# A streaming encoder step on one core: the state recurrence moved ahead of the output tables, and regrouped

## The chip, the cores and the metric

The kernel runs on one core of a Trainium2 chip. The metric is the device time of one execution in microseconds; 879.08 us is the median of three runs of the kernel before (878.42 to 879.44). One more execution was taken by the hardware profiler, and every row below comes from that one.

## What is computed

One layer of a hybrid encoder, for 512 frames of a new stream (the prompt) and 16 frames of each of 8 running streams (the samples), 640 tokens in all. All is float32; a matrix product is made of three products of split halves (high x high, high x low, low x high).

```python
h = rmsnorm(x) @ w_in                      # 1024 x 8192: q, k, v, ga, u, gs, and two gate logits xa, xs
o = softmax(q1 k1) v - lam * softmax(q2 k2) v     # 8 heads, chunk-causal; samples also see 256 cached frames
o = rmsnorm(o) * silu(ga);  ya = o @ w_attn_proj            # "ap"
s_t = a * s_{t-1} + B u_t                  # 64 groups, 64 complex states each
y = gelu(Re(C s) + D u)
y = y * sigmoid(y @ w_glu + b)             # "gl"
ys = (y * silu(gs)) @ w_ssm_proj           # "sp"
x + (sigmoid(xa) * ya + sigmoid(xs) * ys) @ w_out           # "o0", "o1"
```

The recurrence runs by chunks of 8 frames. With a8 the eighth power of a, the state after chunk c is R[c] = R[c] + a8 * R[c-1]: 64 chunks for the prompt, in columns 25 to 88 of R (column 24 is the start), and two chunks for each sample in columns 0 to 15.

## The kernel before, in words

Weights come from DRAM in 512 KB tiles, ScalarE writes their high half (`whi`) and VectorE the rest (`wlo`), and PE multiplies. `gemm_a` makes outputs of 128 tokens by 512 columns, `gemm_b` of 128 columns by 320 tokens. The constant `ORDER` lists the products. Between their matmuls the small steps of attention and of the state space are put in, each a Python generator that yields where it waits. `Weave` is the planner: it keeps an estimated clock for each engine, asks after each group of matmuls whether a generator is due (`poll`), and `DELAY` adds a time to single steps by name. PE's order is the order of the program, planned in this way; the other engines' queues, SP's with all DMAs among them, are ordered by the framework. Engines run their own queues in order.

The state space has these steps:

- `evac_u` splits the product u (`ue`) and stores it to DRAM. `ssm_setup` computes the powers of a in tables `P1`, `P2`, the scaled B in `bbs`, and `a8`.
- `ssm_f` makes 16 tables `F` (three 512-element instructions each, on VectorE or GpSimd, whichever `lighter` finds less loaded). `ssm_in` transposes them on PE, splits them (`Wh`, `Wl`), multiplies with u and stores the chunk inputs (`so`) to `s_d`.
- `ssm_tap` makes 16 tables `E` (three 576-element instructions each, with a helper tile `Et`) and stores them to `e_d`; after each four, 16 matmuls of `E` with `bbs`, 32 columns of the array each, give the taps, which VectorE completes with D and a DMA stores to `tap_d`.
- `states` loads `s_d` into `R` and runs the recurrence; `m` are its helper tiles. `R` goes to `r_d`.
- In the output stage `out_load` brings, for each of 16 groups, `Ef`, `T` (taps), `u` and `H` (states) back; `out_split` splits them into `TO` and `Hs`; `out_mm` runs 24 matmuls (`ps_s<-TO,...`) into `yo`; after two groups `out_gelu` transposes `yo` and applies GELU to `yf`. `y_prep` splits `yf` into `yh`, `yl`, the operand of "gl".

`director` opens and closes the buffers and so sets the stages. Before, `ssm_tap` starts right after `ssm_setup`, beside `ssm_f`; `states` starts when `ssm_in` and `ssm_tap` are done, in the first half of the attention heads. When the heads' inputs and the states are done, the sample phase starts: `sample_k` and `sample_v` load cached keys (`skt`) and values (`svt`) of 512 KB each, `sample_scores` makes scores and softmax (`sw`), `sample_pv` the products with values, whose result `ob` goes to DRAM and comes back as `osm`; `samples_end` norms `osm`, transposes it on PE, multiplies it with its gates (`gaT`) and splits it into the operand of "ap" (`ogh`, `ogl`). The output stage runs beside "ap", and "gl" needs all of its result.

```python
            yield after("ssm_in", 2)                       # director: what follows the input stage
            pclose("wp", "ssm1", "fbuf")
            ...
            if hf == 0:
                yield both(after("tap"), after("att0", ST_AT))
                pclose("tape", "tapp")
                t3 = popen("t3")
                W.add(states(t3))
                yield after("att0", 4)
        yield both(both(after("q0", 5), after("q1", 5)), after("states"))
```

Of the kernel before, what the change touches and what calls it, by code (L numbers as in the profile page):

```python
# [255 lines left out]
def trunk(nc, tc, a):  # L256
# [73 lines left out]
    e_d = dram.tile([128, 64, 144], F32, name="e_d")  # L330
    tap_d = dram.tile([16, 32, 960], F32, name="tap_d")
# [431 lines left out]
    def ssm_tap(tpe):  # L763
        dT = tpe.tile([128, 4, 4], F32, name="dT")
        SP.dma_start(dT, a["dT"])
        dm = tpe.tile([128, 16], F32, name="dm")
# [3 lines left out]
        PL.memset(bbs[:, 64], 0.0)  # L770
# [6 lines left out]
        for q in range(4):  # L777
# [16 lines left out]
            for i in range(4):  # L794
                for g in range(4):
# [267 lines left out]

    def states(t3):
        def cstep(E, dst, src, n):
            sh = [128, 2, 32, n]
            m1, m2 = (t3.tile(sh, F32, name="m12", tag=f"m{n}", bufs=2) for _ in range(2))
            E.tensor_tensor(m1, a8[:, 0, :, :, None].to_broadcast(sh), R[:, :, :, src:src + n], op=OP.mult)
            E.tensor_tensor(m2, a8[:, 1, :, :, None].to_broadcast(sh), R[:, ::-1, :, src:src + n], op=OP.mult)
            E.tensor_tensor(m1, m1, m2, op=OP.add)  # L1070
            E.tensor_tensor(R[:, :, :, dst:dst + n], R[:, :, :, dst:dst + n], m1, op=OP.add)
# [3 lines left out]
        h0 = t3.tile([128, 2, 32, 8], F32, name="h0")  # L1075
        SP.dma_start(h0, a["h0"])
        W.hold()
        yield
        AC.activation(R[:, :, :, 16:24], h0, AF.Copy)
        for d in (8, 0):  # L1080
            for i in range(0, 8, 2):
                cstep(PL, d + i, d + 8 + i, 2)
            yield CHAIN
        PL.tensor_copy(h0, R[:, :, :, 0:8])
        SP.dma_start(a["ss"], h0)
# [317 lines left out]
    def director():  # L1403
# [9 lines left out]
        tpe = popen("tape")  # L1413
# [3 lines left out]
        W.add(ssm_tap(tpe))  # L1417
# [7 lines left out]
        pclose("wp", "ssm1", "fbuf")  # L1425
# [64 lines left out]
    for n, opn, cols in ORDER:  # L1490
# [17 lines left out]
        mark(n)  # L1508
        if n == X_LAST:
# [163 lines left out]
```

## Time and profile before

| what | value |
|---|---|
| median of three runs | 879.08 us |
| the profiled execution, its own time | 887.47 us |
| its span, first to last instruction | 885.7 us |
| mean granted TensorE clock | 0.987 |
| busy: PE, VectorE, ScalarE, GpSimd | 847.1, 558.9, 373.0, 253.0 us |
| DMA | 167.42 MB, mean 189 GB/s |

PE is busy when a matmul is in flight. The stages follow each other in time: v and u to about 105 us, the state-space input with the keys' products to about 237, the first four heads with the recurrence to about 370, the other heads to 523, the samples from 496 to 607, the output stage from 621 to 714, and after that the last four large products alone. The granted clock is a share of the full rate: 1.00 is 2.4 GHz.

### The profile page before, as it was taken

To read this page: it belongs to the slowest core of one execution; us is meant where nothing else is said; L and a number is where in the kernel's file an instruction comes from. 1 tells how busy PE (TensorE), PEld (TensorE's weight loads), DVE (VectorE), ACT (ScalarE), POOL (GpSimd) and SP (SyncE) were. 2 spreads that over 40 slices of the span, in tenths; PEclk is the share of its full clock that TensorE was granted. 3 is DMA by queue.
4 is the path that set the end of the run, shared out by engine and by line. 5 is a ranking of instruction groups with operands and counts; after the bars stand their busy time and mean duration, and the time that the engine had idled before them with its cause. 6 is when DMAs were issued, how large, how long until landed. Compare 5 with 4: busy or idle time off the path is not lost.

```text
span 885.7 us, 15567 instructions
## 1 busy us (share of the span) xinstructions
PE 847.1 (96%) x5692; PEld 776.9 (88%) x5692; DVE 558.9 (63%) x1267; ACT 373.0 (42%) x784; POOL 253.0 (29%) x426
## 2 busy tenths in 40 slices
PE   8999899889899989989999999999999999999998
PEld 6898889789789888767899887789999999999886
DVE  6688449886857788575667764224577755555321
ACT  6432227444236455233555544433565643422110
POOL 3734435323022996879810120000000000000000
PEclk8999899999899999999999999999999999999999
DMA  7365747564818531352585499958989763355231
GB/s 301 97 196 165 224 149 231 163 222 161 263 53 276 161 114 52 102 164 65 170 312 182 155 294 370 353 183 245 290 261 299 226 237 117 105 150 181 95 120 60
DMA packets 96445, 167.42 MB, mean 189 GB/s; under 512 B 16752, under 2 KB 54256, under 8 KB 96112
## 3 DMA queue, kind: packets, MB, share of 16 engines
q1 hardware_dynamic: 96368, 166.42, 59.1%
q8 instruction: 45, 0.74, 0.3%
q14 instruction: 32, 0.26, 0.1%
HBM read 118.45 MB, written 43.75 MB: 183 GB/s over the span
## 4 chain that ended last, share of the span: by engine, by line
PE 62%; POOL 12%; DMA 10%; DVE 10%; issue 3%; ACT 2%; SPq 1%; POOLq 0%; DVEq 0%; ACTq 0%
PE ps_mm L243 50%; POOL m L243 6%; PE ps_s L243 6%; DMA wraw<-in_wb_dram 4%; PE ps_pv L243 3%; PE ps_tp L243 3%; POOL R L243 3%; DVE wlo L243 2%; POOL rs L243 1%; ACT whi L243 1%; DMA svt<-in_cv_dram 1%; DMA H<-r_d 1%; DMA Ef<-e_d 1%; DMA u_d<-ue 1%; DVE kTl L243 1%
## 5 line engine op out<-in xcount | busy, mean ns | idle before, releaser
L243 PE MATMUL ps_mm<-xh,whi 128*128 128x320 f32 x640 | 205.5, 321 | 5.5 <-DVE ue L243 5.5
L243 PE MATMUL ps_mm<-xh,wlo 128*128 128x320 f32 x640 | 199.4, 312 | 0.0
L243 PE MATMUL ps_mm<-xl,whi 128*128 128x320 f32 x640 | 199.3, 311 | 0.0
L243 DVE TENSOR_TENSOR wlo<-wraw,whi 128x1024 fp32r<-128x1024 f32 x96 | 119.8, 1249 | 77.7 <-ACT whi L243 77.1
L243 ACT ACTIVATE whi<-wraw 128x1024 fp32r<-128x1024 f32 x96 | 101.6, 1059 | 109.7 <-PE ps_mm L243 79.6
L243 PEld LDWEIGHTS ps_mm<-xh,whi 128*128 128x128 f32 x640 | 121.9, 190 | 10.8 <-DVE ue L243 6.0
L243 PEld LDWEIGHTS ps_mm<-xl,whi 128*128 128x128 f32 x640 | 121.9, 190 | 0.8
L243 PEld LDWEIGHTS ps_mm<-xh,wlo 128*128 128x128 f32 x640 | 121.6, 190 | 0.0
L243 PE MATMUL ps_mm<-whi,xh 128*128 128x512 f32 x240 | 99.0, 412 | 0.9 <-ACT xh L243 0.9
L243 PE MATMUL ps_mm<-wlo,xh 128*128 128x512 f32 x240 | 95.6, 398 | 0.2 <-DVE wlo L243 0.2
L243 PE MATMUL ps_mm<-whi,xl 128*128 128x512 f32 x240 | 95.6, 398 | 0.0
L243 POOL TENSOR_TENSOR m<-a,R 128x64 f32<-128x64 f32 (+1 forms) x132 | 52.1, 418 | 15.4 <-DMA R<-s_d 8.2
L243 PEld LDWEIGHTS ps_mm<-whi,xl 128*128 128x128 f32 x240 | 46.1, 192 | 10.6 <-DVE xl L243 0.6
L243 PEld LDWEIGHTS ps_mm<-wlo,xh 128*128 128x128 f32 x240 | 46.3, 193 | 9.5 <-DVE wlo L243 1.4
L243 PEld LDWEIGHTS ps_mm<-whi,xh 128*128 128x128 f32 x240 | 46.3, 193 | 9.4 <-ACT xh L243 1.2
L243 POOL TENSOR_TENSOR rs<-ss,mhalf 128x8 f32<-128x8 f32 x20 | 32.9, 1645 | 40.8 <-DVE ss L243 40.6
L243 PE MATMUL ps_mm<-ogh,whi 128*128 128x320 f32 x128 | 41.0, 320 | 0.0
L243 PE MATMUL ps_mm<-yl,whi 128*128 128x320 f32 x128 | 39.6, 309 | 0.0
L243 PE MATMUL ps_mm<-yh,wlo 128*128 128x320 f32 x128 | 39.6, 309 | 0.0
L243 PE MATMUL ps_mm<-y2h,whi 128*128 128x320 f32 x128 | 39.6, 309 | 0.0
L243 PE MATMUL ps_mm<-y2h,wlo 128*128 128x320 f32 x128 | 39.6, 309 | 0.0
L243 PE MATMUL ps_mm<-y2l,whi 128*128 128x320 f32 x128 | 39.6, 309 | 0.0
(291 smaller groups left out, 1887.4 us busy)
## 6 DMA issues: line engine op xcount, KB each, us to landing
wraw<-in_wb_dram SPq DMA_DIRECT2D x64, 512.0 KB, 4.5
wraw<-in_wa_dram SPq DMA_DIRECT2D x32, 512.0 KB, 4.1
u<-u_d SPq DMA_DIRECT2D x16, 640.0 KB, 5.4
skt<-in_ckt_dram SPq DMA_DIRECT2D x16, 512.0 KB, 5.4
svt<-in_cv_dram SPq DMA_DIRECT2D x16, 512.0 KB, 8.0
u_d<-ue SPq DMA_DIRECT2D x16, 320.0 KB, 5.1
gate_xa<-gate SPq DMA_DIRECT2D x16, 320.0 KB, 4.1
e_d<-E SPq DMA_DIRECT2D x16, 288.0 KB, 3.4
```

Source lines behind the costliest of these rows:

```text
L243: r = fn(out, *args, **kw)
```

## The change

- `director` starts `states` as soon as `ssm_in` is done, and `ssm_tap` when `states` is done, in the first half of the heads. The sample phase now waits for `ssm_tap` in place of `states`.
- The tables `P1`, `P2`, `bbs` lie in one tile `tab`, which is stored to DRAM (`tab_d`) at the end of the set-up and loaded again by `ssm_tap`.
- `states` squares a8 three times (a16, a32, a64), combines neighbouring columns by pairs, fours and eights, runs seven single steps, and goes back down. A step takes up to `ST_W` = 8 columns (512 elements) in place of one (64) or two.
- The 16 tap matmuls of a block run over the four column groups in the inner loop; D is multiplied once (`dd`) and added to the product in place of four instructions behind the copy.
- `ORDER` is cut into other pieces, with the same products in all, and `DELAY`, `GAPS`, `BIAS` have other values.

```diff
+    tab_d = dram.tile([128, 2 * 576 + 1040], F32, name="tab_d")
...
-    P1 = tpp.tile([128, 64, 9], F32, name="P1")
-    P2 = tpp.tile([128, 64, 9], F32, name="P2")
-    bbs = tpp.tile([128, 65, 16], F32, name="bbs")
+    def tables(pool):
+        t = pool.tile([128, 2 * 576 + 1040], F32, name="tab")
+        return t, *(t[:, x:x + 576].rearrange("p (g j) -> p g j", j=9) for x in (0, 576)), t[:, 1152:].rearrange("p (g n) -> p g n", n=16)
+    tab, P1, P2, bbs = tables(tpp)
...
+        PL.memset(bbs[:, 64], 0.0)
+        SP.dma_start(tab_d, tab)
         mark("setup")
...
     def ssm_tap(tpe):
+        tab, P1, P2, bbs = tables(tpe)
+        SP.dma_start(tab, tab_d)
+        W.hold()
+        yield
...
-            for i in range(4):
-                for g in range(4):
+            for g in range(4):
+                for i in range(4):
                     gb = 16 * q + 4 * i + g
                     PE.matmul(pt[i * 32:i * 32 + 32, g * 128:g * 128 + 128],
...
-            AC.activation(tp, pt.rearrange("p (g j n) -> p j g n", g=4, j=8), AF.Copy)
-            for g in range(4):
-                DV.scalar_tensor_tensor(tp[:, 0, g], dm, dT[:, q, g:g + 1], tp[:, 0, g], op0=OP.mult, op1=OP.add)
+            pj = pt.rearrange("p (g j n) -> p j g n", g=4, j=8)
+            DV.tensor_tensor(tp[:, 0], dd[:, q], pj[:, 0], op=OP.add)
+            AC.activation(tp[:, 1:], pj[:, 1:], AF.Copy)
...
+        A = [a8] + [t3.tile([128, 2, 2, 32], F32, name=f"a{x}") for x in (16, 32, 64)]
...
-        for c in range(25, RC):
-            if (c - 25) % ST_N == 0:
+        up = [(A[x], 24 + (2 << x), 24 + (1 << x), 32 >> x, 2 << x) for x in range(3)]
+        row = [(A[3], 32 + 8 * k, 24 + 8 * k, 1, 1) for k in range(1, 8)]
+        down = [(A[x], 24 + (3 << x), 24 + (2 << x), (32 >> x) - 1, 2 << x) for x in (2, 1, 0)]
+        for Ax, dst, src, n, step in up + row + down:
+            for k in range(0, n, ST_W):
                 yield CHAIN
-                en = W.lighter(ST_B)
-            cstep(en, c, c - 1, 1)
+                cstep(W.lighter(ST_B), Ax, dst + k * step, src + k * step, min(ST_W, n - k), step)
...
-        tpe = popen("tape")
         fb = popen("fbuf")
...
-        W.add(ssm_tap(tpe))
...
-        pclose("wp", "ssm1", "fbuf")
+        pclose("wp", "ssm1", "fbuf", "tapp")
+        t3 = popen("t3")
+        W.add(states(t3))
...
-                yield both(after("tap"), after("att0", ST_AT))
-                pclose("tape", "tapp")
-                t3 = popen("t3")
-                W.add(states(t3))
+                yield after("states")
+                pclose("t3")
+                W.add(ssm_tap(popen("tape")))
                 yield after("att0", 4)
-        yield both(both(after("q0", 5), after("q1", 5)), after("states"))
-        pclose("t3")
+        yield both(both(after("q0", 5), after("q1", 5)), after("tap"))
+        pclose("tape")
```

Three places of the order show what moves. First VectorE in the u stage, before; `ue` are the splits of the product u, which free its PSUM banks, `wlo` the weight splits:

```order
L243 TENSOR_TENSOR F<-F,Ft 128x512
L243 TENSOR_TENSOR E<-P_112,cc 128x576
L243 TENSOR_TENSOR Et<-P_113,cc 128x576
L243 TENSOR_TENSOR wlo<-wraw,whi 128x1024
L243 TENSOR_TENSOR ue<-ps_mm,ue 128x8x24
L243 TENSOR_TENSOR E<-P_112,cc 128x576
L243 TENSOR_TENSOR F<-F,Ft 128x512
L243 TENSOR_TENSOR E<-E,Et 128x576
L243 TENSOR_TENSOR ue<-ps_mm,ue 128x8x40
```

and the same place after the change:

```order
L243 TENSOR_TENSOR F<-F,Ft 128x512
L243 TENSOR_TENSOR wlo<-wraw,whi 128x1024
L243 TENSOR_TENSOR F<-F,Ft 128x512
L243 TENSOR_TENSOR ue<-ps_mm,ue 128x8x24
L243 TENSOR_TENSOR Ft<-tab,bbi 128x512
L243 TENSOR_TENSOR ue<-ps_mm,ue 128x8x40
```

The table work E is gone from here; in all, 10 of its 16 tables run on VectorE in place of 12, and they stand behind the recurrence. Second PE at the end of the samples, before; `ps_pv<-svn,swn` ends the last sample's product with values, `xh`, `xl` are the operand of the weight products:

```order
L243 MATMUL ps_pv<-svt,swt 32x256 x8
L243 MATMUL ps_pv<-svn,swn 32x256 x4
L243 MATMUL ps_mm<-xh_93,whi 128x320
L243 MATMUL ps_mm<-xl_95,whi 128x320
L243 MATMUL ps_mm<-xh_93,wlo 128x320
```

There are 99 such weight matmuls before the transposes of `osm`, and 90 more before the first output group. After the change:

```order
L243 MATMUL ps_s<-skt,qbd_6222 32x272 x8
L243 MATMUL ps_pv<-svt,swt 32x256 x8
L243 MATMUL ps_pv<-svn,swn 32x256 x4
L243 MATMUL ps_tp<-ident,sw 128x128 x2
L243 MATMUL ps_tp<-ident,sw 16x128
L243 MATMUL ps_pv<-svt,swt 32x256 x8
L243 MATMUL ps_pv<-svn,swn 32x256 x4
L243 MATMUL ps_tp<-ident,osm 128x128 x8
L243 MATMUL ps_mm<-ogh_6274,whi 128x320
```

No weight matmul is left between them, and 57 stand before the first output group; they are of "ap" and read what `osm` becomes. Between the last tap block and the first score 900 weight matmuls stood and 150 stand, between the first score and the last product with values 426 and 231. Third PE in the output stage, before, where the last group meets the transposes; one group is eight rows of three:

```order
L243 MATMUL ps_s<-TO,u_8550 80x128 x3
L243 MATMUL ps_s<-TO,Hs 80x128 x3
L243 MATMUL ps_mm<-ogh_6414,whi 128x320
L243 MATMUL ps_mm<-ogl_6416,whi 128x320
L243 MATMUL ps_mm<-ogh_6414,wlo 128x320
```

and after, from the last matmul of "ap" on:

```order
L243 MATMUL ps_mm<-ogh_6275,wlo 128x320
L243 MATMUL ps_s<-TO,u_8091 80x128 x3
L243 MATMUL ps_s<-TO,Hs 80x128 x3
```

Before, 21 to 33 weight matmuls stood between any two of the 16 groups and 30 behind the last. Now the last six groups follow each other with only the eight transposes of `yo` after every second one, and the first matmul of "gl" stands right behind. From the transposes of `osm` to that matmul there were 492 weight matmuls, and there are 312.

## Rows read from the trace of the kernel before

**Rows 1.** The page's totals by engine: busy us, share of the span, instructions

```profile
PE 847.1 (96%) x5692; PEld 776.9 (88%) x5692; DVE 558.9 (63%) x1267; ACT 373.0 (42%) x784; POOL 253.0 (29%) x426
```

**Rows 2.** Busy time by stage: length, then PE, PEld, DVE, ACT, POOL, PEclk, DMA share, GB/s

```profile
60.00:110.00 50.00, 44.49 (x281) 43.74 (x280) 35.66 (x75) 11.64 (x24) 22.03 (x28) 0.93 0.67 189
110.00:240.00 130.00, 119.60 (x814) 111.83 (x813) 101.30 (x197) 55.81 (x127) 41.85 (x37) 0.97 0.62 196
...
300.00:440.00 140.00, 127.50 (x702) 108.86 (x701) 100.43 (x247) 60.58 (x131) 118.53 (x248) 1.00 0.37 108
...
500.00:580.00 80.00, 79.31 (x677) 65.66 (x676) 38.81 (x102) 36.36 (x91) 6.59 (x21) 1.00 0.95 324
...
620.00:712.00 92.00, 90.45 (x836) 89.89 (x835) 62.95 (x131) 54.93 (x106) 0.00 (x0) 1.00 0.88 265
```

**Rows 3.** PE's waits from 60 to 240 us: us in total, times, longest

```profile
PE ps_mm L243 <- DVE ue L243: 5.5, 2, 4.2
PE ps_s L243 <- DVE tap L243: 4.2, 1, 4.2
```

**Rows 4.** 110 to 240 us: busy time of tile E, of tap, and Et's group

```profile
110.00:240.00 130.00, 7.38 (x96) 6.58 (x96) 12.63 (x17) 5.50 (x4) 0.97 0.62 196
110.00:240.00 130.00, 5.67 (x12) 1.80 (x3) 0.00 (x0) 0.97 0.62 196
L243 DVE TENSOR_TENSOR Et<-P,cc 128x576 f32<-128x576 f32 x8 | 6.9, 861 | 0.1
```

**Rows 5.** Groups: count, busy us, mean ns of one; the recurrence and the F sum

```profile
L243 POOL TENSOR_TENSOR m<-a,R 128x64 f32<-128x64 f32 (+1 forms) x132 | 52.1, 418 | 15.4 <-DMA R<-s_d 8.2
L243 POOL TENSOR_TENSOR R<-R,m 128x64 f32<-128x64 f32 x66 | 30.4, 466 | 3.7
L243 POOL TENSOR_TENSOR m<-m,m 128x64 f32<-128x64 f32 x66 | 27.9, 428 | 3.5
L243 POOL TENSOR_TENSOR F<-F,Ft 128x512 f32<-128x512 f32 x7 | 10.2, 1459 | 0.4
```

**Rows 6.** The chain in order of time: start us, length us; tap products, sample scores

```profile
160.49 2.40 PE ps_pv L243 x32
...
507.82 1.05 PE ps_s L243 x16
```

**Rows 7.** Timeline, end of the samples: start us, length us

```profile
592.38 0.39 ACT L243 ACTIVATE ob<-ps_pv 128x256 f32<-128x256 f32 x1 [2.52 <-PE ps_pv L243]
...
601.29 1.23 DVE L243 TENSOR_TENSOR osm<-osm,sosc 128x1024 f32<-128x1024 f32 x1 [1.84 <-POOL sosc L243]
607.46 1.41 DVE L243 SCALAR_TENSOR_TENSOR gaT<-ps_tp,sub,gaT 128x512 f32<-128x512 f32 x2 [3.55 <-PE ps_tp L243]
608.91 1.35 DVE L243 TENSOR_TENSOR ogl<-gaT,ogh 128x512 fp32r<-128x512 f32 x2
```

**Rows 8.** Output stage: two groups in the chain, a group's splits, last transposes and yl

```profile
613.56 0.62 ACT L243 ACTIVATE TO<-T 128x512 fp32r<-128x512 f32 x1
615.46 0.69 DVE L243 TENSOR_TENSOR TO<-Ef,TO 128x512 fp32r<-128x512 f32 x1
...
621.06 1.71 PE ps_s L243 x24
...
708.18 1.71 PE ps_s L243 x24
712.14 0.56 PE ps_tp L243 x8
717.07 0.82 DVE L243 TENSOR_TENSOR yl<-yf,yh 128x640 fp32r<-128x640 f32 x1
```

**Rows 9.** A stretch behind a wait, columns as in rows 2; weight splits at 110 and 600 us

```profile
80.00:100.00 20.00, 15.80 (x91) 15.54 (x90) 15.03 (x24) 3.88 (x8) 10.58 (x12) 0.83 0.64 180
...
L243 DVE TENSOR_TENSOR wlo<-wraw,whi 128x1024 fp32r<-128x1024 f32 x13 | 17.1, 1317 | 5.6 <-ACT whi L243 5.4
...
L243 DVE TENSOR_TENSOR wlo<-wraw,whi 128x1024 fp32r<-128x1024 f32 x26 | 31.9, 1226 | 17.8 <-ACT whi L243 17.5
```

More of the change, by code (lines that the diff above doesn't have):

```diff
@@ L769, in ssm_tap @@
         PL.tensor_tensor(dm, dm, ident[:, 96:112], op=OP.add)
-        PL.memset(bbs[:, 64], 0.0)
+        dd = tpe.tile([128, 4, 4, 16], F32, name="dd")
+        sh = [128, 4, 4, 16]
+        DV.tensor_tensor(dd, dm[:, None, None, :].to_broadcast(sh), dT[:, :, :, None].to_broadcast(sh), op=OP.mult)
         tpz = tpe.tile([128, 15, 4, 16], F32, name="tap")
@@ L1064, in states, with cstep @@
     def states(t3):
-        def cstep(E, dst, src, n):
+        def cstep(E, A, dst, src, n, step=1):
             sh = [128, 2, 32, n]
-            m1, m2 = (t3.tile(sh, F32, name="m12", tag=f"m{n}", bufs=2) for _ in range(2))
-            E.tensor_tensor(m1, a8[:, 0, :, :, None].to_broadcast(sh), R[:, :, :, src:src + n], op=OP.mult)
-            E.tensor_tensor(m2, a8[:, 1, :, :, None].to_broadcast(sh), R[:, ::-1, :, src:src + n], op=OP.mult)
+            cols = [slice(x, x + step * (n - 1) + 1, step) for x in (dst, src)]
+            m1, m2 = (t3.tile([128, 2, 32, ST_W], F32, name="m", tag="m", bufs=2)[:, :, :, :n] for _ in range(2))
+            E.tensor_tensor(m1, A[:, 0, :, :, None].to_broadcast(sh), R[:, :, :, cols[1]], op=OP.mult)
+            E.tensor_tensor(m2, A[:, 1, :, :, None].to_broadcast(sh), R[:, ::-1, :, cols[1]], op=OP.mult)
             E.tensor_tensor(m1, m1, m2, op=OP.add)
-            E.tensor_tensor(R[:, :, :, dst:dst + n], R[:, :, :, dst:dst + n], m1, op=OP.add)
+            E.tensor_tensor(R[:, :, :, cols[0]], R[:, :, :, cols[0]], m1, op=OP.add)
         R = t3.tile([128, 2, 32, RC], F32, name="R")
         SP.dma_start(R, s_d.rearrange("h p r g c -> (h p) r g c"))
-        h0 = t3.tile([128, 2, 32, 8], F32, name="h0")
+        h0 = t3.tile([128, 2, 32, 8], F32, name="h0", tag="m", bufs=2)
         SP.dma_start(h0, a["h0"])
+        A = [a8] + [t3.tile([128, 2, 2, 32], F32, name=f"a{x}") for x in (16, 32, 64)]
+        sq = t3.tile([128, 32], F32, name="sq")
+        for x, y in zip(A, A[1:]):
+            re, im = x[:, 0, 0], x[:, 1, 1]
+            DV.tensor_tensor(sq, im, im, op=OP.mult)
+            DV.tensor_tensor(y[:, 0, 0], re, re, op=OP.mult)
+            DV.tensor_tensor(y[:, 0, 0], y[:, 0, 0], sq, op=OP.subtract)
+            DV.tensor_scalar(y[:, 0, 1], y[:, 0, 0], 1.0, None, op0=OP.mult)
+            DV.scalar_tensor_tensor(y[:, 1, 0], re, -2.0, im, op0=OP.mult, op1=OP.mult)
+            DV.scalar_tensor_tensor(y[:, 1, 1], re, 2.0, im, op0=OP.mult, op1=OP.mult)
+            yield CHAIN
         W.hold()
@@ L1080, in states @@
         for d in (8, 0):
[L1081 to L1085, printed above, removed]
-        for c in range(25, RC):
-            if (c - 25) % ST_N == 0:
-                yield CHAIN
-                en = W.lighter(ST_B)
-            cstep(en, c, c - 1, 1)
+            for i in range(0, 8, ST_W):
+                cstep(PL, a8, d + i, d + 8 + i, ST_W)
+                yield CHAIN
+        h1 = t3.tile([128, 2, 32, 8], F32, name="h1", tag="m", bufs=2)
+        PL.tensor_copy(h1, R[:, :, :, 0:8])
+        SP.dma_start(a["ss"], h1)
+        up = [(A[x], 24 + (2 << x), 24 + (1 << x), 32 >> x, 2 << x) for x in range(3)]
[3 more added lines that the diff above has]
+            for k in range(0, n, ST_W):
+                yield CHAIN
+                cstep(W.lighter(ST_B), Ax, dst + k * step, src + k * step, min(ST_W, n - k), step)
         last = t3.tile([128, 2, 32], F32, name="last")
@@ L1507, in trunk @@
             gemm_b(op, evacs[n], cols, *((3, lambda i: after("og" if i else "og0")) if n == "ap" else ()))
-        mark(n)
-        if n == X_LAST:
+        if n in ("u", "ap"):
+            mark(n)
+        if (n, cols) == X_LAST:
             mark("xdone")
@@ L1552 @@
 LATENCY = {"PE": 0.28, "AC": 0.2, "DV": 0.06, "PL": 0.3, "SP": 0.1}
-GAPS = 1.3, 0.8, 0.4, 0.2
+GAPS = 1.3, 0.8, 0.0, 0.2
 SB = 3
 WT = 2
-ST_AT = 0
-ST_N = 2
+ST_W = 8
 ST_B = 0.0
@@ L1566 @@
 VH = 6
-X_LAST = "xs"
 WRAW = 2
@@ L1570 @@
 FT = 2
-BIAS = 2.0
+BIAS = 1.36
 WARM = 10
@@ L1578, in cols @@
     return [(n[0], n[1], range(*n[2:])) for n in names]
-ORDER = [("vA", "x", None), ("u", "x", range(8)), ("kA", "x", None), ("ga", "x", range(8)), ("qA", "x", None),
-         ("gs", "x", range(0, 7)), ("kB", "x", None), ("qB", "x", None), ("vB", "x", None), ("gs", "x", range(7, 8)), ("xa", "x", range(0, 8)), ("xs", "x", range(0, 8)),
-         ("ap", "og", range(8)), ("gl", "y", range(8)), ("sp", "y2", range(8)),
+ORDER = [("vA", "x", None), ("u", "x", range(0, 8)), ("kA", "x", None), ("ga", "x", range(0, 8)), ("qA", "x", None),
+         ("gs", "x", range(0, 2)), ("xa", "x", range(0, 1)), ("gs", "x", range(2, 7)), ("kB", "x", None),
+         ("qB", "x", None), ("vB", "x", None), ("xa", "x", range(1, 4)), ("xs", "x", range(0, 1)),
+         ("gs", "x", range(7, 8)), ("xa", "x", range(4, 5)), ("xs", "x", range(1, 3)), ("xa", "x", range(5, 8)),
+         ("xs", "x", range(3, 8)), ("ap", "og", range(0, 8)), ("gl", "y", range(0, 8)), ("sp", "y2", range(0, 8)),
          ("o0", "m", None), ("o1", "m", None)]
+X_LAST = [(n, cols) for n, operand, cols in ORDER if operand == "x"][-1]
 OUTS = {"y": (TOK, 1024), "nk": (TOK, 1024), "nv": (TOK, 1024), "sp": (128, 2, 32), "ss": (128, 2, 32, 8)}
```

65 rows, old and new, of the table DELAY are left out of this document.

## The prediction

> **What bounds it now.** First the page's totals: PE is busy for 847.1 us, 96% of the span [rows 1]. So only PE's idle time, a lower clock, or PE work done quicker can move the end. Then busy time by stage [rows 2]: in each row the first number is the length, then PE's busy time, and PEclk is the granted clock. From 60 to 110 us PE is idle for 5.5 us and the clock of 0.93 takes 7% of 50 us, 3.5 us more: 9.0 us lost. From 110 to 240 it is 10.4 idle and 3% of 130, 3.9: 14.3 us. From 300 to 440 it is 12.5 us at full clock. Together 35.8 us. From 500 to 580 and from 620 to 712 us PE loses 2.2 us in 172, though the DMA share is 0.95 and 0.88: these stages are covered by weight products that stand between their small steps.
>
> PE's waits say why the early stages lose [rows 3]: on the splits of u (5.5 us) and on the taps (4.2 us). VectorE is busy 101.30 of 130 us there. The tables E take 12.63 us of it, the other product Et 6.9, the taps 5.67 [rows 4]: 25.2 us that the change takes out of this stage. From 300 to 440 GpSimd is busy 118.53 of 140 us, which is the recurrence.
>
> **The change, part by part.** I give what each part does to PE's time in the profiled execution. Its own time is 887.47 us, 8.39 us above the median of 879.08, so I add the sum to the median.
>
> *Tables out of the u stage.* The order shows E, Et and E of two groups ahead of a split of u; in the changed order only F work stands there. The first stall of 1.5 us, 15 us before, belongs to the set-up and stays. Of 9.0 us I let 2.5 stay: **-6.5** (bounds 0 and -9.0).
>
> *Tables and taps out of the ssm_in stage.* VectorE's 101.3 us fall by 25.2 and rise by one more F (three instructions, some 2.5 us): 79 us. PE's own work is 130 less 14.3, less three tap blocks of 2.40 [rows 6]: 108 us. VectorE stops being what ends last over the whole, but in the dense part (the splits of so, Wl and F are all there) it stays close, so I let 5 of 14.3 us stay: **-9.5** (0 to -14.3).
>
> *The recurrence.* Before: 52.1 + 30.4 + 27.9 = 110.4 us of GpSimd for 66 dependent steps of four instructions [rows 5]. After: GpSimd has 14 steps of some 512 elements and 7 of 64, VectorE two. At 1459 ns per wide instruction (the F sum, the nearest row) and 1.3 to 1.5 us apart, 56 x 1.46 + 7 x 1.7 = 94 us, begun some 35 us of PE work earlier, beside heads of the first half. Nothing on PE reads it until the output stage. The powers a16, a32, a64 are 18 VectorE instructions of 32 elements, hidden in the 22% that VectorE is idle; without that cover they cost some 4 us.
>
> *Tables into the attention stage.* Ten of 16 tables now run on VectorE (30 instructions at 6.9/8 = 0.86 us, 26 us) and six on GpSimd, between the keys of the second half and the end of its heads. VectorE is busy 100.43 of 140 us there [rows 2], and the recurrence no longer holds GpSimd in front of the norms' powers. The two pull against each other: **-5.5** of the 12.5 us (bounds -12.5, all gone, and +4, the table work uncovered).
>
> *The stores and loads of the tables.* 128 x 2192 floats, 1.1 MB, go out once and come back once, on SP's queue with weights and stores behind them. DMA shares are 0.67 and 0.37 there; the weights are converted up to five tiles ahead, 512 KB per some 7 us. 0, with +4 as the bound if a weight tile is late.
>
> *Tap products with the loops swapped.* Now 16 matmuls of 128 columns take 2.40 us with the same 32-column group four times in a row. The sample scores, whose groups alternate, take 1.05 us for eight of 272 columns [rows 6], where the chain counts two for each. Per column that is 1.17 against 0.48 ns, so a block takes 0.99 us: four blocks, **-5.6** (0 if nothing overlaps).
>
> That is -27.1 early. Now what is late next. The tables end after the first half's recurrence, and the sample phase starts only after them. In the changed order 900 weight products between the last tap block and the first score become 150; from the first score to the first product of the GLU 1,017 become 543. One takes 0.145 us (20 us over 138), so 147 us of cover become 79, while the small steps' chain stays as long. Four places:
>
> *Sample loads.* When the first score runs, four K tiles and six V tiles are there; 12 and 10 tiles of 524 KB are still to come, 11.5 MB, with about 7 MB of weights, gates and small tiles. At the 324 GB/s of this phase or the 265 of the next [rows 2] 18.5 MB need 57 or 70 us. PE has 231 products (33.5 us) and some 21 us of its own: 2.5 or 15.5 us are left, and I take a value nearer the phase's own rate, **+5** (0 to +15).
>
> *End of the samples.* No weight product stands between the last value product and the transposes of osm, where 99 stood. From the copy ob at 592.38 to the normed osm at 602.52 it is 10.1 us, and from the gates after the transposes at 607.46 to their last split at 610.26 it is 2.8 [rows 7]. PE has nothing else in either: **+13** (10 to 14).
>
> *The last six output groups.* The product "ap" is used up after the eleventh group. A group needs its splits (613.56 to 616.15, 2.6 us), then 1.71 us of PE that frees the only set of split buffers, and hand-overs: 4.7 us. Before, groups came every (708.18 - 621.06)/15 = 5.8 us [rows 8]. PE's own is 1.71 and half a transpose of 0.56, so it idles 2.7 to 3.8 us, five times: 13.5 to 19, **+15**. A clock that falls in these gaps adds up to 4 us: from 80 to 100 us, after a wait of 4.2, the clock was 0.83 [rows 9], 17% of some 25 us. The rule on this, "TensorE: Matmul & The Clock Gate" of the Trainium skill, Part 1, is that the array drops to half rate after idling and regains it only by sustained work; by it the groups would run at half rate throughout, about 10 us more. The row is what I take.
>
> *Tail.* From the last transposes (712.14) to the split yl (717.89) it is 5.75 us [rows 8], with the copy yo and hand-overs ahead 6.7; the first 21 GLU products don't need it: **+3**.
>
> Late: +36. Sum: **+8.9 us, 888.0**.
>
> **The rivals.** *Faster, by VectorE's relief.* In the ssm_in and attention stages VectorE is what PE waited for. If it drops below PE everywhere, all but 3 us of the 35.8 go, the tap blocks give 5.6, and the late places come at their low ends (0 + 10 + 13.5 + 3 = 26.5): 867. It decides at the point where the early gain passes the late loss, some 36 us. For it: the table work is 25 of 101 us in the worst stage. Against: those 26 us come back in the attention stage.
>
> *No change.* Early -32 against late +32: 879. The moves then only trade places.
>
> *Slower still, by GpSimd's wide steps.* VectorE's weight split, which reads two SBUF tiles, took 1226 ns on average with GpSimd idle and 1317 with GpSimd busy a third of the time on wide F work [rows 9]: 0.09 us, so some 0.27 if it were always busy. With 30 such instructions beside the recurrence that is 8 us of VectorE, mostly hidden. If GpSimd blocked VectorE for a whole instruction, half of 1.46 us each time, 30 x 0.73 = 22 us, of which some 10 reach PE: 898. This is the rule of "SBUF — State Buffer" in the Trainium skill, "Who interferes with whom": one of the two holds the shared port for a full instruction and the other blocks. The rows show an eighth of it.
>
> **Chances.** The forecast 0.50; faster by relief 0.30; no change 0.08; slower by the port 0.12. A difference under 0.2% (1.8 us) can't be told from none. So faster 0.30, same 0.08, slower 0.62. The range 866 to 901 takes in the relief's figure and the port's, and leaves out both tails, some 0.2. The forecast's own range is 880 to 898.
>
> **What would show it.** Right: PE idle under 4 us from 60 to 110 and some 5 from 110 to 240; each tap block about 1 us; a gap of some 13 us between the last value product and the first "ap" product after osm; six output groups 4.7 us or more apart with PE idle between; GLU's first product some 724 us into the span. Wrong: if the groups come under 4 us apart, if ssm_in's stalls stay, or if scores stand still for loads by more than 15 us.

## The result, and the profile after

The changed kernel takes 923.45 us (median of four runs, 921.46 to 924.62) beside 878.75 us for the kernel before: a ratio of 1.0506, 95% interval 1.0483 to 1.0529. It is slower by 45 us where I said 9, and outside the range. The profiled execution's own time is 924.48 us. The totals of its page:

```profile
span 922.6 us, 15383 instructions
...
PE 857.1 (93%) x5692; PEld 781.1 (85%) x5692; DVE 581.7 (63%) x1255; ACT 373.8 (41%) x784; POOL 248.0 (27%) x249
```

Busy time by stage, columns as in [rows 2]; the first two stages, the stage of the attention heads in one piece and then in two, the end of the samples, and the last output groups:

```profile
60.00:110.00 50.00, 49.24 (x315) 47.55 (x315) 33.01 (x74) 12.51 (x26) 10.18 (x16) 1.00 0.72 206
110.00:220.00 110.00, 102.60 (x683) 97.42 (x682) 80.80 (x174) 52.98 (x121) 32.70 (x30) 0.97 0.59 179
219.00:572.00 353.00, 328.80 (x2062) 296.32 (x2061) 255.74 (x544) 152.37 (x343) 164.70 (x143) 0.98 0.54 172
219.00:360.00 141.00, 128.97 (x766) 116.77 (x766) 111.98 (x241) 59.80 (x147) 111.39 (x97) 0.96 0.39 120
360.00:572.00 212.00, 199.83 (x1297) 179.55 (x1296) 143.76 (x303) 92.58 (x196) 53.31 (x46) 1.00 0.64 206
635.00:647.00 12.00, 0.96 (x10) 0.28 (x3) 2.62 (x3) 1.44 (x2) 1.64 (x1) 0.50 0.64 197
647.00:660.00 13.00, 12.20 (x65) 11.45 (x65) 6.63 (x11) 4.79 (x7) 0.00 (x0) 0.74 0.31 89
722.00:750.00 28.00, 19.34 (x141) 17.50 (x141) 16.63 (x40) 15.21 (x31) 0.00 (x0) 0.68 0.79 240
```

The first two rows answer to the first two of [rows 2]: PE is idle for 0.8 us in place of 5.5, and for 7.4 of 110 us in place of 10.4 of 130. The heads' stage is where the forecast broke: PE stands for 24.2 of 353 us, and half of that, 12.0 us, in the 141 us up to 360, where GpSimd is busy for 111 us, mostly with the recurrence. In the kernel before, profiled again (first experiment), PE stood there for 12.6 of 260 us:

```profile
234.00:494.00 260.00, 247.44 (x1451) 218.72 (x1453) 186.14 (x486) 123.14 (x289) 147.17 (x299) 0.99 0.48 150
```

The last three rows of the changed kernel are what I had expected late: a gap of 11 us, a clock of 0.74 behind it, and last groups in which PE is busy for 19.3 of 28 us at 0.68.

For a comparison by stage I use one measure in all that follows, and call it PE's loss: for each pair of successive matmuls the time between their starts, less the median of that time for the same shape in the first trace of before (for the 32-column products, whose intervals alternate, 30 ns for taps, 64 and 65 for the samples), summed over a stage. It counts idle time and a low clock alike. The kernel before was profiled once more (first experiment) and stands in the first column; its span there is 880.3 us, so the two spans differ by 42.3.

| stage, from one PE instruction to another | before | changed | difference | my terms |
|---|---|---|---|---|
| start to the first transpose of F | 13.1 | 7.9 | -5.2 | -6.5 |
| to the last state-space input product | 16.7 | 10.0 | -6.7 | -9.5, three tap blocks -4.2 |
| to the first sample score | 22.7 | 37.1 | +14.4 | -5.5, one tap block -1.4 |
| to the last product with values | 3.2 | 6.3 | +3.1 | +5 |
| to the first output group | 0.3 | 15.7 | +15.4 | +13 |
| to the first product of the GLU | 0.8 | 20.8 | +20.0 | +15, +3 |
| to the end | -0.3 | 1.0 | +1.3 | 0 |
| sum | 56.5 | 98.8 | +42.3 | +8.9 |

The late terms hold in sum: +36 forecast, +39.8 measured. The early ones don't: -27.1 forecast, +2.5 measured.

### The profile page after: what moved, and what is told of

It is laid out like the page before. It is cut to its first block, busy times and chain, and to the rows that moved or that the text cites. A ratio compares the mean times of both kernels' runs of the same rounds, so it can differ in the third digit from the quotient of the medians.

```text
span 922.6 us, 15383 instructions
## 1 busy us (share of the span) xinstructions
PE 857.1 (93%) x5692; PEld 781.1 (85%) x5692; DVE 581.7 (63%) x1255; ACT 373.8 (41%) x784; POOL 248.0 (27%) x249
## 5 line engine op out<-in xcount | busy, mean ns | idle before, releaser
L243 PE MATMUL ps_mm<-xh,whi 128*128 128x320 f32 x640 | 203.4, 318 | 2.5 <-DVE ss L243 1.7
L243 DVE TENSOR_TENSOR wlo<-wraw,whi 128x1024 fp32r<-128x1024 f32 x96 | 122.1, 1274 | 88.6 <-ACT whi L243 78.3
L243 PEld LDWEIGHTS ps_mm<-whi,xh 128*128 128x128 f32 x240 | 47.1, 196 | 11.2 <-ACT xh L243 1.4
L243 POOL TENSOR_TENSOR rs<-ss,mhalf 128x8 f32<-128x8 f32 x20 | 35.5, 1774 | 67.7 <-DVE ss L243 61.0
L243 POOL TENSOR_TENSOR m<-a,R 128x512 f32<-128x512 f32 (+2 forms) x42 | 45.6, 1106 | 2.1 <-DMA out_ss_dram<-h 1.4
L243 PE MATMUL ps_mm<-ogl,whi 128*128 128x320 f32 x128 | 40.4, 316 | 0.2 <-DVE ogl L243 0.2
L243 PE MATMUL ps_mm<-yh,whi 128*128 128x320 f32 x128 | 40.2, 314 | 0.0
L243 PE MATMUL ps_mm<-ogh,wlo 128*128 128x320 f32 x128 | 40.1, 314 | 0.0
```

What stands on the lines that cost most here:

```text
L243: r = fn(out, *args, **kw)
```

## The experiments

Every time stands beside the kernel before on the same chip, whose median there was 881.4 to 882.2 us; so ratios are compared, the changed kernel's being 1.0506.

**Before, once more.** No edit.

> The kernel before, unchanged, profiled once more. Its profiled execution took 887.47 us, the runs without a look 878 to 879; the changed kernel's profiled execution took 924.48 against a median of 923.45. Theory: the first profiled execution held some 8 us of waits that most executions don't have, so the 9.0 us that I read as lost from 60 to 110 us were in part not there to win. Then this execution takes 879 to 881 us and loses under 4 us from 60 to 110 us. Rival: the profiler itself costs this kernel 8 us; then 887 again, with the same waits at 71.8 and 87.5 us.

Measured: 881.19 us (ratio 0.9994, 0.9966 to 1.0021), profiled span 880.3. The loss up to the last state-space input product is 29.8 us, 33.8 in the first profile, and PE's two waits for the splits of u, at 72 and 88 us, are 1.7 and 3.0 us, 1.3 and 4.2 there. So the profiler costs nothing that shows here, and the first profile held some 5 us that this execution doesn't have (spans 885.7 and 880.3 us), 4.0 of them in the first two stages. My 35.8 us of early loss were too many by about as much.

**The recurrence on VectorE.**

```diff
-                cstep(PL, a8, d + i, d + 8 + i, ST_W)
+                cstep(DV, a8, d + i, d + 8 + i, ST_W)
-ST_B = 0.0
+ST_B = 1000.0
```

> The changed kernel with every step of the recurrence on VectorE. Theory (port): GpSimd's steps of 512 elements lengthen those VectorE instructions that read two SBUF tiles (sb<-s,c,sb takes 1.19 us on average beside them, 0.59 before), and that makes the attention stage lose 37 us of PE time where before it lost 21. Without GpSimd in it, sb comes back to 0.6 us, the recurrence ends before 310 us in place of 356, tables and samples start some 40 us earlier, and the whole takes 890 to 912 us. Rival (queue): VectorE is simply too full; 21 steps of four instructions at 0.69 us are 50 us more for it, PE's waits grow, and the time is 923 us or more.

Measured: 940.71 us, ratio 1.0664 (1.0617 to 1.0712). The rival's outcome: the loss of the heads' stage rises to 54.2 us, VectorE is busy for 271 of 349 us. But the theory's first sign is there too. Groups by line on VectorE while the recurrence runs, with wide steps on GpSimd in the changed kernel, and then with all steps on VectorE, each shape by itself; `sb<-s,c,sb` reads two SBUF tiles, `sb<-ps_s,dist` one and PSUM:

```profile
L243 DVE SCALAR_TENSOR_TENSOR sb<-s,c,sb 128x256 f32<-128x256 f32 x4 | 6.1, 1536 | 0.0
L243 DVE SCALAR_TENSOR_TENSOR sb<-s,c,sb 128x128 f32<-128x128 f32 x4 | 3.6, 912 | 0.1
L243 DVE CUSTOM_DVE_ANT_0 sb<-ps_s,dist 128x256 f32<-128x256 f32 x4 | 1.6, 409 | 0.0
```

```profile
L243 DVE SCALAR_TENSOR_TENSOR sb<-s,c,sb 128x256 f32<-128x256 f32 x4 | 1.9, 476 | 0.0
L243 DVE SCALAR_TENSOR_TENSOR sb<-s,c,sb 128x128 f32<-128x128 f32 x4 | 1.4, 343 | 0.0
```

With 256 elements it falls from 1536 to 476 ns, with 128 from 912 to 343; in the kernel before, beside 64-element steps, these took 532 and 426, and `sb<-ps_s,dist` of 256 elements 420, so that one didn't move. Both things are so: beside wide GpSimd work this instruction takes twice its time (1228 ns on average over its four shapes, 611 in the kernel before), and with the recurrence on VectorE as well PE loses more, not less.

**The regrouped recurrence alone, in its old place.** The function `states` of the change in the kernel before.

> The kernel before, with the recurrence by pairs, fours and eights in its old place and nothing else. Theory (port): sb<-s,c,sb beside it goes from 0.59 to 1.0 us or more, PE's loss between the state-space input and the first sample score rises from 22 to some 32 us, nothing waits for the recurrence's earlier end, and the time is 886 to 894 us. Rival: VectorE has room for it, 878 to 883 us. Second rival: the shorter recurrence lets the samples start earlier, under 877 us.

Measured: 911.06 us, ratio 1.0336 (1.0288 to 1.0385): 30 us from this one part, more than the theory said. The loss up to the first score is 42.4 us, 22.7 without it, and `sb` takes 1.14 us on average. In the profiled execution these 19.7 us are most of the 25.5 by which its span is longer; 4.3 lie behind the first product of the GLU, where I didn't look for the cause.

**The same with thin steps.**

```diff
-                cstep(W.lighter(ST_B), Ax, ..., min(ST_W, n - k), step)
+                cstep(W.lighter(ST_B), Ax, ..., 1, step)
```

> The kernel before with the regrouped recurrence in its old place, as in the run that took 911 us, but every one of the 21 prompt steps works on one column (64 elements) in place of up to eight (512); the number of instructions, their chain and the place stay, most columns keep the chunk inputs. Theory (width): sb<-s,c,sb comes back from 1.14 to 0.6 us, PE's loss from the state-space input to the first score from 42 to 20 to 26 us, 877 to 886 us. Rival (order): the planner's hand-set delays fit another sequence of steps, and that is what cost 30 us; then the loss stays over 33 us and the time over 893 us.

Measured: 876.13 us, ratio 0.9937 (0.9917 to 0.9958); loss 11.8 us. Same 21 steps, same chain, same place, but in the 14 wide steps one column in place of up to eight, so most of the recurrence is left out: 35 us less. PE's waits in that stage, with wide steps and then with thin ones (us in total, times, longest):

```profile
PE ps_tp L243 <- DVE sb L243: 8.4, 3, 3.9
PE ps_tp L243 <- DVE qn L243: 4.2, 1, 4.2
PE ps_tp L243 <- DVE orz L243: 4.1, 1, 4.1
```

```profile
PE ps_tp L243 <- DVE sb L243: 3.3, 3, 1.5
PE ps_tp L243 <- DVE o L243: 1.2, 1, 1.2
```

The order of the steps is thus not what cost 30 us. Since the thin run also moves fewer elements, the next one separates width from load.

**Idle GpSimd work beside the last products**, in the kernel before:

```diff
+        p, q = OPS["dum"]
+        for _ in range(n):
+            nc.gpsimd.tensor_tensor(p[:, :w], p[:, :w], q[:, :w], op=OP.mult)
...
+        beside(5, 512)
...
+        beside(15, 64)
```

> The kernel before with work on GpSimd that nobody reads, in the last 160 us where GpSimd is idle: beside each output of gl five products of 512 elements, beside each output of sp fifteen of 64. The weight split wlo<-wraw,whi takes 1.21 to 1.23 us there with GpSimd idle. Theory (width): beside the wide products it takes 1.5 us or more, beside the narrow ones 1.35 us or less, though GpSimd is about as busy. Rival: both stretch it alike, since both keep GpSimd busy. PE is covered there, so the time stays within 878 to 885 us either way.

Measured: 947.0 us (two runs, 946.53 and 947.47), ratio 1.075. By shape, VectorE from 720 to 835 us in the kernel before, profiled again, with GpSimd idle:

```profile
L243 DVE TENSOR_TENSOR wlo<-wraw,whi 128x1024 fp32r<-128x1024 f32 x15 | 18.4, 1226 | 12.6 <-ACT whi L243 12.6
L243 DVE SCALAR_TENSOR_TENSOR sg<-sg,yf 128x320 f32<-128x320 f32 x14 | 6.8, 489 | 0.1
L243 DVE SCALAR_TENSOR_TENSOR xs<-xs,ps_mm 128x320 f32<-128x320 f32 x16 | 7.8, 487 | 18.4 <-PE ps_mm L243 18.4
```

GpSimd and VectorE in the same stretch while the wide products ran:

```profile
L1370 POOL TENSOR_TENSOR dum<-dum,dum 128x512 f32<-128x512 f32 x72 | 110.7, 1538 | 5.6
L243 DVE TENSOR_TENSOR wlo<-wraw,whi 128x1024 fp32r<-128x1024 f32 x11 | 24.8, 2257 | 0.0
L243 DVE SCALAR_TENSOR_TENSOR sg<-sg,yf 128x320 f32<-128x320 f32 x15 | 23.6, 1575 | 0.0
L243 DVE SCALAR_TENSOR_TENSOR xs<-xs,ps_mm 128x320 f32<-128x320 f32 x8 | 3.8, 475 | 0.0
```

and while the narrow ones ran (850 to 930 us):

```profile
L1370 POOL TENSOR_TENSOR dum<-dum,dum 128x64 f32<-128x64 f32 x188 | 65.9, 351 | 14.7
L243 DVE TENSOR_TENSOR wlo<-wraw,whi 128x1024 fp32r<-128x1024 f32 x5 | 6.5, 1291 | 6.5 <-ACT whi L243 6.5
L243 DVE TENSOR_TENSOR ml<-xs,mh 128x320 fp32r<-128x320 f32 x3 | 1.7, 569 | 0.5 <-ACT mh L243 0.5
```

With GpSimd idle the split takes 1226 ns and `sg<-sg,yf` 489. Beside products of 512 elements they take 2257 and 1575: some 1.05 us more for each, two thirds of one GpSimd instruction of 1.54. The other instructions there with two SBUF inputs pay 0.46 to 0.96 us. Beside products of 64 elements the split takes 1291, 65 ns more: the price falls to a sixteenth, where the elements that GpSimd works per microsecond fall to about half (320 and 150). `xs<-xs,ps_mm`, which reads PSUM and one SBUF tile, takes 475 against 487: untouched. The theory holds, and I was wrong that PE is covered there: VectorE became the bound and PE lost 32 us. The other 33 us of the longer time are GpSimd's own, which was still at its narrow products when PE had ended (the last matmul begins at 907.7 of 944.7 us).

**The changed kernel without the prompt's recurrence steps.** The loop over `up + row + down` runs over nothing.

> The changed kernel without the 21 steps of the recurrence for the prompt (the states of the prompt stay the chunk inputs; the sample steps stay). Theory (port): with no wide steps on GpSimd, sb<-s,c,sb comes back to 0.6 us, PE's loss from the state-space input to the first score falls from 37 to 22 us or less, and the tables begin 100 us sooner, so 186 weight matmuls stand before the transposes of osm: 15 and 16 us less, 888 to 897 us, with the last six groups bare as they are. Rival (tables): the table work on VectorE is what makes the stage lose; then its loss stays over 30 us and the time is 900 to 910 us.

Measured: 896.76 us, ratio 1.0167 (1.0142 to 1.0193), 30 us less. The loss up to the first score is 26.1 us, a little over the theory's 22 and 11.0 less than with the steps, so the tables alone cost the stage little. The tables also begin sooner, and the end of the samples is covered: 0.3 us lost before the transposes of osm. What this run still loses late is mostly the bare groups: 19.0 us.

**The tables' loads ahead.**

```diff
-                SP.dma_start(cc, a["cC"][b].rearrange(...))
-                W.hold()
+                cc, there = ccs.pop(0)
+                if b + 3 < 16:
+                    load_cc(b + 3)
+                W.hold(there)
...
-                yield room("pv") if i == 3 else None
+                yield room("pv") if i == 3 else CHAIN
```

> The changed kernel with the loads of the tables' C three ahead, in place of each waited for. Theory: the samples start late because 16 tables follow each other with a load in front of each, 155 us from the first to the last tap block; so 150 weight products are left for the scores and none for the end of the samples. With loads ahead 978 matmuls of the weights in place of 1,323 stand before the last tap block and 120 before the transposes of osm in place of 0. The 11.6 us gap and the 4.1 us behind it at a lower clock go, the last six groups stay bare: 905 to 911 us. Rival: the tables in a shorter stretch fill VectorE's and GpSimd's queues, the attention stage loses 10 us more, and the time is 915 to 924 us.

Measured: 911.5 us, ratio 1.0347 (1.0314 to 1.038), as the theory said. The gap is gone; PE in that place, columns as above:

```profile
616.00:634.00 18.00, 18.00 (x126) 17.86 (x123) 5.52 (x7) 3.16 (x5) 2.51 (x1) 1.00 0.66 216
```

Of the late 40 us some 18 go with the taps' lateness, and the heads lose 3 us more: 14 us less in all.

**The same with the late delays of before.** The entries of `DELAY` for samples and output groups are those of the kernel before.

> As the run with the tables' loads ahead, and the planner's delays for the samples and the output stage as in the kernel before. Its order keeps 96 weight matmuls before the transposes of osm and leaves three output groups bare in place of six. Theory (cover): each bare group costs 2.5 to 3 us, clock included, so 8 us less than that run: 896 to 903 us. Rival: the groups are slow for their loads or splits wherever they stand; then no difference to that run.

Measured: 906.0 us, ratio 1.0283 (1.0249 to 1.0316). Some 6 us less, with three bare groups in place of six. The loss from the first output group to the GLU is 15.8 us, 19.5 in the run above: the cover counts, by less per group than I said.

**Two sets of split buffers** (`TOB = 2` in place of 1, in the changed kernel).

> The changed kernel with two sets of split buffers for the output groups in place of one. Theory: the last groups come 5.3 us apart because a group's splits wait for the products of the group before; with two sets the pace falls to what VectorE and ScalarE need, 3.5 to 4 us, the last six groups give 7 to 10 us, with a higher clock behind, and the time is 910 to 917 us. Rival: the loads or the engines set the pace; the groups stay over 5 us apart and the time stays within 921 to 925 us.

Measured: 920.25 us, ratio 1.0431 (1.0379 to 1.0482). The loss from the twelfth group to the GLU falls from 18.4 to 8.8 us, but 5.1 of that come back before it, where groups now come earlier than their cover. The set of buffers paces the bare groups, and it is a small part.

**PE kept busy in the gaps** (in the changed kernel).

```diff
+    def keep(n):
+        ps = ps_mm()
+        for _ in range(n):
+            nc.tensor.matmul(ps[:, :128], ident, ident, start=True, stop=True)
...
         yield room("tp", 2)
+        keep(44)
...
+                if 2 * ct + i >= 11:
+                    keep(9)
```

> The changed kernel with idle products on PE (of the unit matrix, read by nobody): 44 in front of the transposes of osm, 9 in front of each of the last five output groups. Theory (clock): of the 36 us that PE loses from the last value product on, some 13 us are a granted clock of 0.66 to 0.83 behind the gaps; with PE kept busy in the gaps the clock stays at 1.00 and the time falls by 8 to 14 us, to 910 to 916 us. Rival: what paces those stretches is the small steps on VectorE and ScalarE, whatever the clock; then 921 us or more, for the idle products can also be late.

Measured: 922.27 us, ratio 1.0462 (1.0432 to 1.0493), an interval that overlaps the changed kernel's. The clock comes back and most of the time doesn't. The idle products (88 records, 11.8 us), then two rows by stage:

```profile
632.28 11.82 PE L1252 MATMUL ps_mm<-ident 128*128 128x128 f32 x88
```

```profile
640.00:660.00 20.00, 18.62 (x148) 18.15 (x148) 11.12 (x16) 7.68 (x12) 1.64 (x1) 1.00 0.55 159
720.00:740.00 20.00, 17.26 (x143) 16.84 (x142) 11.40 (x28) 11.09 (x22) 0.00 (x0) 0.74 0.79 225
```

From 640 to 660 us the clock is 1.00, 0.66 in the changed kernel; from the transposes of osm to the first group it takes 11.2 us in place of 13.3. From the twelfth group to the GLU it is 28.8 us in place of 28.7. So the low clock was worth some 2 us at the first place, and at the second nothing that this run could get back, since the idle products stand in the way themselves (18 records, 2.2 us at full clock, in front of a group).

**Swapped tap loops, alone.** The two `for` lines of the tap products, in the kernel before.

> The kernel before with the two loops of the tap products swapped and nothing else. Theory: each of four blocks takes 0.9 us on PE in place of 2.3 us (in the changed kernel they do), they stand where PE is the bound, and the time falls by 4 to 6 us, to 873 to 875. Rival: PE waits for VectorE around them anyway; the blocks get shorter, the waits longer, and the time stays within 878 to 880 us.

Measured: 880.58 us, ratio 0.9983 (0.9959 to 1.0007): the rival. A block takes 1.0 us in place of 2.4 (in the changed kernel the timeline shows this):

```profile
429.56 1.08 PE L243 MATMUL ps_pv<-E,tab 128*32 128x128 f32 x32
```

but the wait behind the third block is longer by 1.9 us. PE's waits there, in the kernel before, profiled again, and with the swap:

```profile
PE ps_s L243 <- DVE tap L243: 2.7, 1, 2.7
```

```profile
PE ps_s L243 <- DVE tap L243: 4.6, 1, 4.6
```

**The whole edit of the tap block, alone** (loops, `dd`, and one addition from PSUM).

> The kernel before with the whole edit of the tap block (loops swapped, D multiplied once, one addition from PSUM) and nothing else. The swap alone shortened each block by 1.4 us, and the wait for tap behind the third block grew from 3.0 to 4.9 us. Theory: that wait is for the copy and the four instructions with D on VectorE; with one addition straight from PSUM it falls to 2 us or less, PE keeps the 5.6 us of the blocks, and the time is 4 to 8 us below the kernel before on the same chip. Rival: VectorE is late there for its other work; no difference beyond 2 us.

Measured: 883.61 us, ratio 1.0021 (1.0 to 1.0042). The wait for tap is gone; PE waits for `so` for 10.8 us in place of 5.3. The rival: VectorE is late there for its other work.

**Tables E after the product u.** `W.add(ssm_tap(tpe))` moved behind `yield after("u")`.

> The run with the tap block's edit, and the tables E started after the product u in place of beside it. Theory: the waits of 1.8 and 3.2 us for the splits of u and the lower clock behind them come from three table instructions that stand ahead of a split; with them gone the stretch from 60 to 110 us loses 2 us in place of 7, the taps end some 15 us later and nothing waits for that: 4 to 6 us less than the tap block's edit alone. Rival: the table work comes back in the state-space input stage, where VectorE is busy for 101 of 130 us, and its waits take the 5 us away again.

Measured: 899.06 us, ratio 1.0195 (1.0171 to 1.0219). The edit didn't do what it says. VectorE's timeline at the old stall still has the tables in front of the split:

```profile
84.99 0.76 DVE L243 TENSOR_TENSOR E<-P,cc 128x576 f32<-128x576 f32 x1 [0.54 <-DMA cc<-in_cC_dram]
85.67 1.73 DVE L243 TENSOR_TENSOR Et<-P,cc 128x576 f32<-128x576 f32 x1
87.32 2.12 DVE L243 TENSOR_TENSOR wlo<-wraw,whi 128x1024 fp32r<-128x1024 f32 x1
89.36 0.34 DVE L243 TENSOR_TENSOR ue<-ps_mm,ue 128x192 fp32r<-128x192 f32 x1
```

The framework orders VectorE's queue and put them there all the same; that it places them as early as their inputs allow would fit, and wasn't tried. The wait stayed (4.6 us), and the next two stages lost 11 us more. The run says nothing on its theory.

**Thin tables**, without and with the swapped loops, in the kernel before: on GpSimd each instruction of `ssm_f` and `ssm_tap` becomes four over one group each, and `BIAS = 1.0`.

> The kernel before, where GpSimd's share of the tables F and E (some 6 and 4 of 16 each) is worked in instructions of 128 and 144 elements, four for one of 512 and 576, and the bias between the engines is 1.0 in place of 2.0 so that the shares stay about as they were. Theory (width): these wide instructions are what makes VectorE late with the splits of u and with so; thin ones give VectorE 5 to 10 us back between 60 and 240 us, PE's loss there falls by 3 to 8 us, 873 to 878 us beside some 881 for the kernel before. Rival: GpSimd needs half as long again for them, its tables come late, and the time is 881 us or more.

> The same with the two loops of the tap products swapped. Theory: if VectorE is no longer what PE waits for there, the 5.6 us that the four blocks get shorter reach the end: 4 to 6 us less than the run with thin tables alone. Rival: the wait behind the blocks grows by as much again, as it did without the thin tables; no difference beyond 2 us.

Measured: 893.4 us, ratio 1.0132 (1.01 to 1.0164), and 890.41 us, ratio 1.0101 (1.0068 to 1.0133). A miss. The u stage loses 2.6 us less, but the state-space input 27.2 us in place of 16.7: PE waits for `so` for 11.2 us. The two differ by less than their intervals, so nothing is shown on the loops.

**Single steps in the new place**, with the loads ahead and the late delays of before.

> The changed kernel with the tables' loads ahead and the late delays of before (the run that took 906 us), and the recurrence in 64 single steps as in the kernel before, in its new early place. Theory (width): PE's loss from the state-space input to the first score falls from 44 to 25 to 30 us; but the chain is longer, the taps end later, the order has no weight matmul before the transposes of osm again (96 in that run) and five bare groups in place of three, which costs 10 to 16 us: 900 to 910 us, the gain traded for the late loss. Rival: the loss in the stage stays over 38 us, and the time goes over 915 us.

Measured: 944.7 us, ratio 1.0708, and the loss up to the first score is 48.8 us. A miss, though `sb` is back at 0.60 us while the steps run and PE is idle for only 4.4 of 80 us from 300 to 380. The time went behind it. One wait of 8.75 us, and VectorE in front of it:

```profile
418.71 0.66 PE L243 MATMUL ps_tp<-ident,qn 128*128 128x128 f32 x2 [8.75 <-DVE qn L243]
```

```profile
408.40 0.75 DVE L243 TENSOR_TENSOR E<-tab,cc 128x576 f32<-128x576 f32 x1
410.12 0.74 DVE L243 TENSOR_TENSOR E<-E,Et 128x576 f32<-128x576 f32 x1
411.57 0.74 DVE L243 TENSOR_TENSOR E<-tab,cc 128x576 f32<-128x576 f32 x1
412.23 0.74 DVE L243 TENSOR_TENSOR Et<-tab,cc 128x576 f32<-128x576 f32 x1
414.70 0.74 DVE L243 TENSOR_TENSOR E<-E,Et 128x576 f32<-128x576 f32 x1
```

Table instructions stand between the pieces of the norm that ends in `qn`. With the chain later, the tables meet the queries' norms; and the samples begin late again, with no cover for osm. How much a delay table made for this order would give back was not tried.

## Why the prediction was wrong

**The step that failed is the recurrence, and with it the attention stage.** I costed the steps as GpSimd time ("Nothing on PE reads it until the output stage"), and gave the stage -5.5 us, with a tap block of -1.4. It lost 14.4: 21.3 of the 33.4 us between forecast and measurement by the table, where the state-space input stage has 7.0, the late places 3.8 and the u stage 1.3. The price is not GpSimd's time but what a wide GpSimd instruction does to VectorE: in the old place, with nothing else changed, regrouping costs 30 us, and with thin steps 35 us less than that; and in the new place the loss falls by 11.0 us without the steps. It fits that the stage's first 141 us, beside the recurrence, hold 12.0 us of idle time at a clock of 0.96, and the next 212 us, with the tables in them, 12.2 us at full clock.

I had this mechanism as a rival and priced it away. From the weight split's mean of 1226 and 1317 ns [rows 9] I took 0.09 us and scaled it to 0.27; as the worst case I took half a wide instruction, 0.73 us. Either price I put on 30 table instructions alone, and gave 898 us and a chance of 0.12. Both halves failed. The mean hid the price, and the same trace showed it: of the 13 splits behind 1317 ns eleven took 1.21 to 1.23 us, and two, beside GpSimd's F work, took 1.56 and 2.13:

```profile
141.85 1.56 DVE L243 TENSOR_TENSOR wlo<-wraw,whi 128x1024 fp32r<-128x1024 f32 x1
200.34 2.13 DVE L243 TENSOR_TENSOR wlo<-wraw,whi 128x1024 fp32r<-128x1024 f32 x1
```

With GpSimd busy on wide work throughout, a split pays 1.03 us on average. And the recurrence stands beside all of VectorE's work on two SBUF tiles: the splits, `sb`, even the one-element `c`. "SBUF — State Buffer" in the Trainium skill, "Who interferes with whom", says that a VectorE instruction with two SBUF inputs contends with a GpSimd instruction that reads SBUF, and one with a single SBUF input, outside VectorE's two-port modes, doesn't. The runs agree on both: 2257 against 1226 ns for the split, 475 against 487 with PSUM as one input. I had set that rule against an average in which two instructions of 13 show it.

**The state-space input stage** gave 6.7 us where I had 13.7 with its tap blocks. The blocks got shorter as I worked out (1.0 us), and nothing came of it: alone, the swap moved the time by nothing that can be measured, because PE's waits for VectorE there grew (for tap from 2.7 to 4.6 us). I had put the blocks on PE's path and VectorE's work on its own, and counted both.

**The u stage** was right (-5.2 for -6.5; idle 0.8 us, under the 4 us I named), with E out of the splits' way. That this is the cause rests on the order and the trace: the run that was to show it alone didn't do it, and GpSimd lost its share of E there as well. Some of what I read as lost was this one profiled execution's: 4.0 of 33.8 us up to the last state-space input product.

**The late terms** were right in sum and in place, but not in what they are made of: the gap at the end of the samples +15.4 with the slower stretch behind it for +13, the output groups and the tail +20.0 for +18, the samples' loads +3.1 for +5. PE stood for 11.0 us before the transposes of osm and 0.8 behind them, where I had 10.1 and 2.8; the clock of 0.74 in the 13 us that follow, 3.4 us more by the prediction's own reading, I had put at nothing. The bare groups came 5.5 us apart (721.7 to 743.7 in four), over my 4.7, but by turns some 7 and 4 us. In the 28 us of the last groups PE is idle for 8.7 us, where I had 13.5 or more in the groups and 3 in the tail, and a clock of 0.68 stands for some 9 us by the same reading, where I allowed up to 4 from one row at 0.83. So +18 came near by two sizes that were off against each other, which is luck. "TensorE: Matmul & The Clock Gate" in the Trainium skill, Part 1, with an array at half rate after idling, gave about 10 us there by the prediction's estimate, and the trace, at 0.68 and not at half throughout, is nearer to that than to my row. What it would be worth to hold the clock is another matter: in the run with idle products it brought back 2 us behind the first gap, and inside the bare groups that run can't say.

**The cause behind the late terms** was shown for the gap: with the tables' loads ahead, the samples come sooner, the gap closes, and 14 us go. Most of the rest of the late loss lies at the six groups without cover; 4 to 7 us of it went with either edit that I tried on them.

No version came out measurably below the kernel before with the whole computation in it. The thin run, which leaves most of the recurrence out, gives an upper estimate of what a recurrence without its width could be worth in that place: some 5 us.

## What to carry to other kernels

Before work on GpSimd is called hidden, look at what VectorE does beside it: in these runs each VectorE instruction with two SBUF inputs paid for up to two thirds of a wide GpSimd instruction (0.46 to 1.09 us of 1.54), while 64-element ones cost it next to nothing (65 ns of 1226). A regrouping that has fewer but wider steps can therefore lose on another engine what it gains in its own chain. A price from a mean is worth little if few of the instructions behind it met the cause, and a gain on one engine and one on the engine that it waits for must not both be added.

## What the runs showed of the hardware that I had not expected

- The size of the effect of width: beside GpSimd products of 512 elements (95% busy) VectorE's split went from 1226 to 2257 ns, a 320-element product from 489 to 1575; beside products of 64 (82% busy) the split took 1291. Even a one-element instruction, `c<-z,neglam,c`, went from 290 to 572 ns on average in the changed kernel.
- GpSimd's own instructions vary as well: its additions of 512 elements took 1.33 and 1.84 us within 8 us of each other in the recurrence. That VectorE holds it up in turn would fit, and was not tried.
- Thirty-two-column tap products that change the column group each time took 1.0 us in a block that took 2.4 us with four in a row on one group.
- Keeping PE busy with idle products brought the granted clock from 0.66 to 1.00 in a stretch and gained 2 us there; at the bare groups the time was the same with them, 28.8 and 28.7 us.
